# A gated linear recurrence on Trainium2: its in-block products as 32-column tiles of the TensorE array

## The chip, the cores and the metric

The kernel runs on one core of a Trainium2 chip. A core has a matrix engine (TensorE; PE in the profile, with its weight loads shown separately as PEld), a vector engine (VectorE, DVE), a scalar engine (ScalarE, ACT), a general engine (GpSimd, POOL) and a queue that issues DMAs (SyncE, SP). Each engine works through its own list of instructions in order and waits on semaphores for the others. The metric is the device time of one execution in microseconds (us), the median of the runs.

## The reference, cut to what matters

The kernel computes one layer of a diffusion backbone for 1024 latent and 128 context tokens of width 1024: a half-step SwiGLU network, a token mixer, a second half-step SwiGLU network and a final norm. The mixer adds attention and a bidirectional gated linear recurrence (HGRN2) with 8 heads of 64 x 64 state:

```
S_t = diag(f_t) S_{t-1} + k_t outer v_t        k_t = 1 - f_t
o_t = S_t^T q_t
```

It runs once forward and once backward over the latent tokens, each from a cached start state, and once over the context tokens from zero. The reference does it in chunks: inside a chunk the products are

```
A[t, s] = sum_k  decay(s -> t)[k] q[t, k] k[s, k]     (s <= t forward, s >= t backward)
o_intra[t] = sum_s A[t, s] v[s]
dS = sum_s (k[s] decayed to the chunk's end) outer v[s]
```

and between chunks the state goes on as `S <- diag(g) S + dS`, with `o_inter[t] = (q[t] decayed from the chunk's start) S`.

## The kernel before, in words

All matrix data stands feature-major: 128 features on the partitions, the 1152 tokens (1024 latent, 128 context) along the free axis, cut into three column groups of 384, taken in the order `ORDER = (2, 0, 1)`. The large dense products split every fp32 operand into a high and a low part and run three matmuls for it (`mm3`, lines 446 to 448; one record each). Small products stay in plain fp32; the profile shows each of these as two weight loads and two matmul records, except transposes, which are one of each.

The work goes: `start` and `ffn_fast` (first SwiGLU), `hgrn` (recurrence, with the dense projections that feed it and others woven in), `attn`, `merge`, and `ffn_fast` again. The change is in `hgrn` alone.

For each of the 8 heads the recurrence keeps forward data on partitions 0 to 63 (slice `A`) and backward data on 64 to 127 (slice `B`). One head has three units of 384 tokens, each of three blocks of 128 tokens. So there are 24 units. A unit is worked in two generators.

`scan_pre` makes keys and queries relative to blocks of 8 tokens (`Kb`, `Qb`), and `KE` and `QP`, their versions decayed to the ends of the 8-token blocks.

`scan_lev` then makes the 128 x 128 matrix of `A[s, t]` of each of the three blocks.

- First the 8-token blocks: line 858 multiplies `Kb` by `Qb` over the forward rows (a contraction of 64) into one PSUM tile of the tag `lv` and over the backward rows into another, three matmuls of 128 x 128 each. Line 859 copies what an 8-block mask lets through into `A1` and `A2` (VectorE, `copy_predicated`, 128 x 384).
- Then four levels m = 8, 16, 32, 64. `key_half` (lines 864 and 865, ScalarE) copies the left-half keys of each pair of m-blocks for forward and the right-half keys for backward into `kr`, whose other halves are zero. Line 873 multiplies `kr` by `QP` over all 128 rows, three matmuls of 128 x 128. Line 884 moves `KE` (two VectorE instructions) and `QP` (one GpSimd, one VectorE) on to blocks of 2m, and line 885 the factors `T`. For m < 64, line 888 copies what the mask of this level lets through from PSUM into `A1`; for m = 64, lines 890 and 891 copy the two off-diagonal quarters (ScalarE).
- Line 895 adds `A1` and `A2` to `Af` (VectorE, 128 x 384). Line 899 transposes `KE`, line 901 copies that out of PSUM, line 905 multiplies it by all 128 columns of `V` (two heads' values) and line 906 keeps the 64 of this head as `dS`.

After the three units of a head, `scan_out` runs the state through the blocks (line 916, 14 VectorE instructions) and then, for each unit, accumulates `V^T Af` (line 924) and `S^T QP` (line 928) into a PSUM tile `po`, on those 64 partitions that belong to the head, and copies them out (line 929).

Every generator yields between its steps. The loop in `hgrn` takes, at each yield of `scan_lev` or `scan_out`, one step of dense projection work (twelve matmuls of lines 446 to 448) and one step of `scan_pre` of the next unit. So TensorE's list reads: a small group of the recurrence, twelve dense matmuls, the next small group, and so on. A scheduler then settles the final order of each engine's list. PSUM tiles: the tag `lv` has three buffers, `sm` (transposes, `dS`, `po`) three and `mm` (dense) two.

Of the kernel before, what the change touches and what calls it, by code (L numbers as in the profile page):

```python
# [9 lines left out]
F32 = mybir.dt.float32  # L10
F32R = mybir.dt.float32r
BF16 = mybir.dt.bfloat16
U8 = mybir.dt.uint8
# [6 lines left out]
P = 128  # L20
# [6 lines left out]
CW = 384  # L27
# [3 lines left out]
ORDER = (2, 0, 1)  # L31
FINAL = (768, 1152), (0, 512), (512, 768)
H = 8
EPS = 1e-6
# [53 lines left out]
class Trunk:  # L88
# [515 lines left out]
    def mixer_consts(self, cp):  # L604
        nc, a = self.nc, self.a
        self.mask = cp.tile([P, 5, P], U8, name="mask")
        mf = self.tt(F32, "maskf")[:, : 5 * P]
        nc.scalar.dma_start(mf, a["mask"])
# [98 lines left out]
    def hgrn(self):  # L707
        nc = self.nc
# [3 lines left out]
        f32 = lambda n, sh: self.fp.tile(sh, F32, name=n)  # L712
        A, B = slice(0, 64), slice(64, P)
        self.kr = {m: [f32(f"kr{m}_{i}", [P, CW]) for i in range(1)] for m in (8, 16, 32, 64)}
# [3 lines left out]
        for m in self.kr:  # L718
            for t in self.kr[m]:
                nc.vector.memset(t, 0.0)  # L720
        for t in self.XY:
            nc.vector.memset(t[:, :, 3:4], 1.0)
        for t in self.A1 + self.A2:
# [37 lines left out]
        d = scan_of(0)  # L761
# [24 lines left out]
    def tmp(self, n, bufs=1, sh=(P, CW)):  # L786
        return self.fp.tile(list(sh), F32, tag=n, bufs=bufs, name=n)
# [48 lines left out]
    def scan_lev(self, d, b):  # L836
        nc = self.nc
# [9 lines left out]
        dS = d["dS"]  # L847
        A1, A2 = self.A1[self.cnt % 2], self.A2[0]
        self.cnt += 1
        Kb, Qb, KE, Tm = d["pre"]  # L850
        bc = lambda t, m: t.unsqueeze(2).to_broadcast([t.shape[0], t.shape[1], m])
        qp = QP[:, c0 : c0 + CW]
        lv = lambda: self.pp.tile([P, 3, P], F32, tag="lv", bufs=3, name="lv")
        mb = lambda i: self.mask[:, i].unsqueeze(1).to_broadcast([P, 3, P])
        for r, dst, mi in ((A, A1, 0), (B, A2, 1)):
            ps = lv()
            for j in range(3):
                nc.tensor.matmul(ps[:, j], Kb[r, ts(j, P)], Qb[r, ts(j, P)], start=True, stop=True)
            nc.vector.copy_predicated(dst, mb(mi), ps)
# [9 lines left out]
        for li, m in enumerate((8, 16, 32, 64)):  # L869
            kr = self.kr[m][0]  # L870
            ps = lv()
            for j in range(3):
                nc.tensor.matmul(ps[:, j], kr[:, ts(j, P)], qp[:, ts(j, P)], start=True, stop=True)
            tv = Tm.rearrange("p (n h) -> p n h", h=2)
# [11 lines left out]
            if m < 64:  # L886
                key_half(2 * m)
                nc.vector.copy_predicated(A1, mb(2 + li), ps)
            else:
                nc.scalar.copy(A1[A, :, B], ps[A, :, B])  # L890
                nc.scalar.copy(A1[B, :, A], ps[B, :, A])
            Tm = Tn
            yield
        Af = tmp("Af", 4, (P, 3, P))
        nc.vector.tensor_add(Af, A1, A2)
        d["As"][b] = Af
        pt = self.pp.tile([P, 3, P], F32, tag="sm", bufs=3, name="kt")
# [4 lines left out]
        yield  # L902
        pd = self.pp.tile([P, 3, P], F32, tag="sm", bufs=3, name="dS")
        for j in range(3):
            nc.tensor.matmul(pd[:, j], kT[:, j], V[:, ts(3 * b + j, P)], start=True, stop=True)
        nc.scalar.copy(dS[:, 3 * b : 3 * b + 3], pd[:, :, 64 * hh : 64 * hh + 64])
        yield

    def scan_out(self, d):
# [9 lines left out]
        r = slice(off, off + 64)  # L919
        for b in ORDER:  # L920
            po = self.pp.tile([P, 3, P], F32, tag="sm", bufs=3, name="po")
            for j in range(3):
                t = 3 * b + j
                nc.tensor.matmul(
                    po[r, j], V[:, t * P + off : t * P + off + 64], d["As"][b][:, j], start=True, stop=(t == 8)
                )
                if t < 8:
                    nc.tensor.matmul(po[r, j], S[:, t], QP[:, ts(t, P)], start=False, stop=True)
            nc.scalar.copy(d["o"][r, b * CW : (b + 1) * CW], po[r].rearrange("p a b -> p (a b)"))
            yield  # L930
# [836 lines left out]
def mask_table():  # L1767
    import numpy as np

    s, t = np.arange(P)[:, None], np.arange(P)[None, :]  # L1770
    same = lambda b: s // b == t // b
    m = [same(8) & (s <= t), same(8) & (s >= t)]
    m += [same(2 * b) & ~same(b) for b in (8, 16, 32)]
    return np.concatenate(m, 1).astype(np.float32)
# [35 lines left out]
```

## Time and profile before

| | |
|---|---|
| Runs | 2983.42, 2985.15, 2987.38 us; median 2985.15 |
| Profiled execution | 2987.2 us from its first to its last instruction; the page gives no other time for it |
| Mean granted TensorE clock | 0.987 |
| TensorE matmul busy | 2879.0 us (96%), 18498 records |
| TensorE weight loads busy | 2739.4 us (92%) |
| VectorE / ScalarE / GpSimd busy | 2026.6 / 1238.5 / 1029.7 us |
| The recurrence's stage | about 886 to 1508 us of the span |

Busy time of an engine is a union of its records, and matmul records overlap: a record of line 446 lasts about 0.34 us while the next starts 0.175 us after it. What a small group costs is therefore read from start to start in the timeline, not from the length of records.

### The profile page before, as it was taken

Reading aid. Unit: us, or ns where it says so; the run is one execution under the profiler, and the core shown is the slowest. Engines: PE = TensorE matmul, PEld = TensorE weight load, DVE = VectorE, ACT = ScalarE, POOL = GpSimd, SP = SyncE. Lnnn points to the kernel's source line nnn. Section 1 sums busy time; section 2 is a strip of 40 time slices with the busy share of each in tenths; the row PEclk is TensorE's granted clock in tenths of the full one; section 3 lists DMA queues with packets and bytes.
Section 4 is the critical chain, followed back from the end, with each engine's and each line's share of the span. In section 5 each row is a group of like instructions: output and inputs, shape, how many; then the busy total and the mean of one; then the engine's idle time right before and its main releaser. Section 6 shows DMA issues by size and latency. Waiting matters only on the chain. (4 is left out here: it accounts for less than half of the span.)

```text
span 2987.2 us, 49338 instructions
## 1 busy us (share of the span) xinstructions
PE 2879.0 (96%) x18498; PEld 2739.4 (92%) x18498; DVE 2026.6 (68%) x4238; ACT 1238.5 (41%) x2374; POOL 1029.7 (34%) x939
## 2 busy tenths in 40 slices
PE   6999999999989999999998999989999999999998
PEld 5999999999979989898997777779999999999997
DVE  7677777677677777878456677756674665546665
ACT  6432332321364555555244777731462233232112
POOL 0223223453243333323244445532342322226431
PEclk9999999999999999999998999999999999999999
DMA  6643433743121111111110000242352322235211
GB/s 242 205 142 120 133 121 118 265 138 116 63 64 56 38 44 38 54 38 51 60 48 12 16 15 25 62 161 82 123 176 94 106 88 75 74 110 210 91 45 64
DMA packets 151470, 282.37 MB, mean 95 GB/s; under 512 B 19200, under 2 KB 83648, under 8 KB 151232
## 3 DMA queue, kind: packets, MB, share of 16 engines
q1 hardware_dynamic: 151088, 278.90, 28.3%
q8 instruction: 146, 2.39, 0.3%
q14 instruction: 92, 0.75, 0.1%
q10 hardware_dynamic: 144, 0.33, 0.0%
HBM read 215.64 MB, written 63.52 MB: 93 GB/s over the span
## 5 line engine op out<-in xcount | busy, mean ns | idle before, releaser
L1560 PE MATMUL b<-xo,wo 128*128 128x288 f32 x3552 | 484.8, 296 | 0.0
L1560 PEld LDWEIGHTS b<-xo,wo 128*128 128x128 f32 x3552 | 476.6, 188 | 0.0
L475 DVE SCALAR_TENSOR_TENSOR x<-dn,modt,x 128x256 f32<-128x256 f32 (+4 forms) x728 | 353.4, 505 | 169.2 <-PE dn L448 168.1
L235 POOL TENSOR_TENSOR wl<-raw,wh 128x1024 fp32r<-128x1024 f32 (+1 forms) x106 | 235.4, 2222 | 418.7 <-ACT wh L234 353.0
L1560 PE MATMUL b<-bh,wo 128*128 128x288 f32 x1776 | 365.9, 295 | 0.8 <-ACT et L1570 0.8
L446 PE MATMUL mm<-xh,wh 128*128 128x384 f32 (+1 forms) x1008 | 360.5, 358 | 6.1 <-DVE q L665 4.1
L448 PE MATMUL mm<-xh,wl 128*128 128x384 f32 (+1 forms) x1008 | 342.2, 340 | 2.1 <-POOL wl L235 1.9
L447 PE MATMUL mm<-xl,wh 128*128 128x384 f32 (+1 forms) x1008 | 342.0, 339 | 0.0
L1560 PEld LDWEIGHTS b<-bh,wo 128*128 128x128 f32 x1776 | 289.1, 188 | 1.0 <-ACT et L1570 1.0
L1560 PE MATMUL b<-bl,wo 128*128 128x288 f32 x888 | 261.7, 295 | 0.0
L234 ACT CAST wh<-raw 128x1024 fp32r<-128x1024 f32 (+1 forms) x108 | 104.3, 968 | 257.2 <-PE dn L447 165.8
L1535 ACT CAST wo<-raw 128x512 fp32r<-128x512 f32 x185 | 114.7, 621 | 229.0 <-PE b L1560 116.9
L446 PEld LDWEIGHTS mm<-xh,wh 128*128 128x128 f32 (+1 forms) x1008 | 190.2, 189 | 16.0 <-DVE q L665 4.9
L446 PE MATMUL dn<-hh,wh 128*128 128x384 f32 (+2 forms) x576 | 196.3, 341 | 2.0 <-DVE x L475 1.1
L1536 DVE TENSOR_TENSOR wo<-raw,wo 128x512 fp32r<-128x512 f32 x185 | 127.1, 688 | 103.3 <-ACT wo L1535 100.3
L448 PE MATMUL dn<-hh,wl 128*128 128x384 f32 (+2 forms) x576 | 194.7, 338 | 1.0 <-POOL wl L235 1.0
L447 PE MATMUL dn<-hl,wh 128*128 128x384 f32 (+2 forms) x576 | 194.2, 337 | 0.0
L448 PEld LDWEIGHTS mm<-xh,wl 128*128 128x128 f32 (+1 forms) x1008 | 189.7, 188 | 3.6 <-POOL wl L235 2.2
L447 PEld LDWEIGHTS mm<-xl,wh 128*128 128x128 f32 (+1 forms) x1008 | 190.4, 189 | 1.7 <-issue 0.4
L1638 POOL TENSOR_TENSOR hl<-hr,hh 128x1152 fp32r<-128x1152 f32 x44 | 117.9, 2689 | 197.1 <-ACT hh L1637 105.8
L1292 POOL TENSOR_TENSOR ehl<-e,ehl 128x512 fp32r<-128x512 f32 x93 | 122.1, 1318 | 143.8 <-ACT ehl L1290 83.6
L306 DVE SCALAR_TENSOR_TENSOR junk<-wada,cb 128x512 bf16<-128x512 f32 x224 | 165.9, 741 | 5.3 <-DMA wada<-in_w_aT 4.5
(388 smaller groups left out, 7125.0 us busy)
## 6 DMA issues: line engine op xcount, KB each, us to landing
raw<-in_w SPq DMA_DIRECT2D x148, 256.0 KB, 2.9
raw<-in_w SPq DMA_DIRECT2D x58, 512.0 KB, 3.7
wada<-in_w_aT SPq DMA_DIRECT2D x112, 256.0 KB, 2.8
hr<-hs SPq DMA_DIRECT2D x44, 576.0 KB, 5.6
hs<-et SPq DMA_DIRECT2D x148, 144.0 KB, 1.8
raw<-in_w_in SPq DMA_DIRECT2D x41, 512.0 KB, 3.6
hb<-hd SPq DMA_DIRECT2D x44, 288.0 KB, 3.2
x<-in_xT SPq DMA_DIRECT2D x16, 576.0 KB, 6.2
```

The lines of the kernel that those rows point to most:

```text
L234: pin(self.nc.scalar.copy(wh, raw))
L235: pin((eng or self.nc.gpsimd).tensor_sub(wl, raw, wh))
L306: nc.vector.scalar_tensor_tensor(junk, ws[n % 2], 1.0, cs[s], ALU.mult, ALU.mult, accum_out=o)
L446: pin(nc.tensor.matmul(ps, wh, xh, start=start and i == 0, stop=False))
L447: pin(nc.tensor.matmul(ps, wh, xl, start=False, stop=False))
L448: pin(nc.tensor.matmul(ps, wl, xh, start=False, stop=stop and i == n - 1))
L475: nc.vector.scalar_tensor_tensor(self.x[m][:, a:b], ps[:, a - lo : b - lo], self.modt[:, gm, m, s : s + 1], self.x[m][:, a:b], ALU.mult, A ...
L1292: eng.tensor_sub(el, e, eh)
L1535: nc.scalar.copy(wh, src[i])
L1536: nc.vector.tensor_sub(wl, src[i], wh)
L1560: nc.tensor.matmul(ps, w[:, k], x[:, k, :QW], start=first, stop=last, skip_group_check=home != i)
L1638: nc.gpsimd.tensor_sub(hl, raw, hh)
```

## The change

- `mixer_consts`, `mask_table`: with the new constant `G = 32`, the masks are four of 128 x 32 in place of five of 128 x 128; column c of row s stands for token 32 * (s // 32) + c.
- `scan_lev`, products inside 32-token blocks (the 8-blocks and the levels 8 and 16): a new helper `products` issues, for each of the three blocks of 128, a 32 x 32 matmul for each of the four 32-token diagonal blocks, with the output on that block's own 32 partitions. For the 8-blocks it does so for the forward rows and the backward rows in turn, into two PSUM tiles.
- Levels 32 and 64: only the blocks that hold results are multiplied, forward over rows `A` into one `lv` tile and backward over rows `B` into another: at level 32 four matmuls of 32 x 32 per block of 128, at level 64 two of 64 x 64. The keys' zero halves are no longer needed there, so only `kr8` and `kr16` are cleared at the start.
- The masked copies and `A1`, `A2` shrink to 128 x 96, and the sum becomes `Ad` (128 x 96). `Af` is filled by ScalarE copies: four of 32 x 96 from `Ad` after level 16, four of 32 x 96 from PSUM at level 32, two of 64 x 192 at level 64.
- `dS`: two 64-column weight halves by the 64 columns of `V` of this head, into the two halves of one PSUM tile.
- `scan_out`: two PSUM tiles for nine blocks in place of three. In each, some blocks go to partitions 0 to 63 and others to 64 to 127, issued alternately; the order of blocks is 3, 4, 2, 5 and then 1, 6, 0, 7, 8. Four copies per head bring them out in place of three, and there is one yield less.

```diff
@@ mixer_consts
-        self.mask = cp.tile([P, 5, P], U8, name="mask")
+        self.mask = cp.tile([P, 4, G], U8, name="mask")
...
@@ hgrn
-        self.A1 = [f32(f"A1_{i}", [P, 3, P]) for i in range(2)]
-        self.A2 = [f32("A2", [P, 3, P])]
+        self.A1 = [f32(f"A1_{i}", [P, 3, G]) for i in range(2)]
+        self.A2 = f32("A2", [P, 3, G])
...
@@ scan_lev
+        Af = d["As"][b] = tmp("Af", 4, (P, 3, P))
...
-        lv = lambda: self.pp.tile([P, 3, P], F32, tag="lv", bufs=3, name="lv")
-        mb = lambda i: self.mask[:, i].unsqueeze(1).to_broadcast([P, 3, P])
-        for r, dst, mi in ((A, A1, 0), (B, A2, 1)):
-            ps = lv()
-            for j in range(3):
-                nc.tensor.matmul(ps[:, j], Kb[r, ts(j, P)], Qb[r, ts(j, P)], start=True, stop=True)
-            nc.vector.copy_predicated(dst, mb(mi), ps)
+        lv = lambda: self.pp.tile([P, 3, 64], F32, tag="lv", bufs=3, name="lv")
+        mb = lambda i: self.mask[:, i].unsqueeze(1).to_broadcast([P, 3, G])
+
+        def products(parts, k, q, blocks):
+            for j in range(3):
+                kj, qj = k[:, ts(j, P)], q[:, ts(j, P)]
+                for ki, qi in blocks:
+                    for r, ps in parts:
+                        ks, qs = (ki, qi) if r != B else (qi, ki)
+                        n = qs.stop - qs.start
+                        nc.tensor.matmul(ps[ks, j, :n], kj[r, ks], qj[r, qs], start=True, stop=True)
+
+        diag = [slice(u, u + G) for u in range(0, P, G)]
+        diag = list(zip(diag, diag))
+        pair = (A, lv()), (B, lv())
+        products(pair, Kb, Qb, diag)
+        for dst, mi, (_, ps) in zip((A1, A2), (0, 1), pair):
+            nc.vector.copy_predicated(dst, mb(mi), ps[:, :, :G])
...
         for li, m in enumerate((8, 16, 32, 64)):
-            kr = self.kr[m][0]
-            ps = lv()
-            for j in range(3):
-                nc.tensor.matmul(ps[:, j], kr[:, ts(j, P)], qp[:, ts(j, P)], start=True, stop=True)
+            kr = self.kr[m]
+            if m < G:
+                ps = lv()
+                products([(slice(0, P), ps)], kr, qp, diag)
+            else:
+                pair = (A, lv()), (B, lv())
+                blocks = [(slice(u, u + m), slice(u + m, u + 2 * m)) for u in range(0, P, 2 * m)]
+                products(pair, kr, qp, blocks)
...
             if m < 64:
                 key_half(2 * m)
-                nc.vector.copy_predicated(A1, mb(2 + li), ps)
+            if m < G:
+                nc.vector.copy_predicated(A1, mb(2 + li), ps[:, :, :G])
             else:
-                nc.scalar.copy(A1[A, :, B], ps[A, :, B])
-                nc.scalar.copy(A1[B, :, A], ps[B, :, A])
+                for u, v in blocks:
+                    nc.scalar.copy(Af[u, :, v], pair[0][1][u, :, :m])
+                    nc.scalar.copy(Af[v, :, u], pair[1][1][v, :, :m])
+            if m == 16:
+                Ad = tmp("Ad", 2, (P, 3, G))
+                nc.vector.tensor_add(Ad, A1, A2)
+                for u, _ in diag:
+                    nc.scalar.copy(Af[u, :, u], Ad[u])
             Tm = Tn
             yield
-        Af = tmp("Af", 4, (P, 3, P))
-        nc.vector.tensor_add(Af, A1, A2)
-        d["As"][b] = Af
...
-        pd = self.pp.tile([P, 3, P], F32, tag="sm", bufs=3, name="dS")
+        pd = self.pp.tile([P, 3, 64], F32, tag="sm", bufs=3, name="dS")
         for j in range(3):
-            nc.tensor.matmul(pd[:, j], kT[:, j], V[:, ts(3 * b + j, P)], start=True, stop=True)
-        nc.scalar.copy(dS[:, 3 * b : 3 * b + 3], pd[:, :, 64 * hh : 64 * hh + 64])
+            for r in (A, B):
+                v = V[:, (3 * b + j) * P + 64 * hh : (3 * b + j) * P + 64 * hh + 64]
+                nc.tensor.matmul(pd[r, j], kT[:, j, r], v, start=True, stop=True)
+        nc.scalar.copy(dS[:, 3 * b : 3 * b + 3], pd)
...
@@ scan_out
-        for b in ORDER:
+        for pairs, lows, highs in (((3, 4), (2, 5)), (2, 4), (4, 6)), (((1, 6), (0, 7), (8,)), (0, 2), (6, 9)):
             po = self.pp.tile([P, 3, P], F32, tag="sm", bufs=3, name="po")
-            for j in range(3):
-                t = 3 * b + j
-                nc.tensor.matmul(
-                    po[r, j], V[:, t * P + off : t * P + off + 64], d["As"][b][:, j], start=True, stop=(t == 8)
-                )
-                if t < 8:
-                    nc.tensor.matmul(po[r, j], S[:, t], QP[:, ts(t, P)], start=False, stop=True)
-            nc.scalar.copy(d["o"][r, b * CW : (b + 1) * CW], po[r].rearrange("p a b -> p (a b)"))
+            at = lambda t: po[A, t - lows[0]] if t < lows[1] else po[B, t - highs[0]]
+            for pair in pairs:
+                for t in pair:
+                    w = V[:, t * P + off : t * P + off + 64]
+                    nc.tensor.matmul(at(t), w, d["As"][t // 3][:, t % 3], start=True, stop=(t == 8))
+                for t in pair:
+                    if t < 8:
+                        nc.tensor.matmul(at(t), S[:, t], QP[:, ts(t, P)], start=False, stop=True)
+            for half, (t0, t1) in ((A, lows), (B, highs)):
+                pv = po[half, : t1 - t0].rearrange("p a b -> p (a b)")
+                nc.scalar.copy(d["o"][r, t0 * P : t1 * P], pv)
             yield
```

In the built program a unit's five product groups hold 24, 12, 12, 12 and 6 matmuls in place of 6, 3, 3, 3 and 3, `dS` has 6 in place of 3, and a head's outputs keep 17. ScalarE's list has ten `Af` copies per unit in place of the two of lines 890 and 891. The dense matmuls, the loads and the stores are the same in number.

More of the change, by code (lines that the diff above doesn't have):

```diff
@@ L32 @@
 FINAL = (768, 1152), (0, 512), (512, 768)
+G = 32
 H = 8
@@ L605, in mixer_consts @@
         nc, a = self.nc, self.a
[L606 to L607 removed]
+        self.mask = cp.tile([P, 4, G], U8, name="mask")
+        mf = self.tt(F32, "maskf")[:, : 4 * G]
         nc.scalar.dma_start(mf, a["mask"])
@@ L713, in hgrn @@
         A, B = slice(0, 64), slice(64, P)
-        self.kr = {m: [f32(f"kr{m}_{i}", [P, CW]) for i in range(1)] for m in (8, 16, 32, 64)}
+        self.kr = {m: f32(f"kr{m}", [P, CW]) for m in (8, 16, 32, 64)}
         self.XY = [f32(n, [P, 48, 8]) for n in "XY"]
-        self.A1 = [f32(f"A1_{i}", [P, 3, P]) for i in range(2)]
-        self.A2 = [f32("A2", [P, 3, P])]
-        for m in self.kr:
-            for t in self.kr[m]:
-                nc.vector.memset(t, 0.0)
+        self.A1 = [f32(f"A1_{i}", [P, 3, G]) for i in range(2)]
+        self.A2 = f32("A2", [P, 3, G])
         for t in self.XY:
             nc.vector.memset(t[:, :, 3:4], 1.0)
-        for t in self.A1 + self.A2:
+        for t in self.A1 + [self.A2, self.kr[8], self.kr[16]]:
             nc.vector.memset(t, 0.0)
@@ L1768, in mask_table @@
     import numpy as np
-    s, t = np.arange(P)[:, None], np.arange(P)[None, :]
+    s = np.arange(P)[:, None]
+    t = s // G * G + np.arange(G)[None, :]
     same = lambda b: s // b == t // b
     m = [same(8) & (s <= t), same(8) & (s >= t)]
-    m += [same(2 * b) & ~same(b) for b in (8, 16, 32)]
+    m += [same(2 * b) & ~same(b) for b in (8, 16)]
     return np.concatenate(m, 1).astype(np.float32)
```

4 lines of the change are left out of this document (2 added, 2 removed).

## The prediction

> **What bounds the kernel now.** I read the page's totals, then the busy times of the recurrence's stage, its TensorE groups and waits, then timelines. First the page's totals; then stage rows (start:end, length, busy time of PE, PEld, DVE, ACT, POOL, granted clock): the stage and two heads of it.
>
> ```profile
> span 2987.2 us, 49338 instructions
> PE 2879.0 (96%) x18498; PEld 2739.4 (92%) x18498; DVE 2026.6 (68%) x4238; ACT 1238.5 (41%) x2374; POOL 1029.7 (34%) x939
> ```
>
> ```profile
> 1197.00:1275.00 78.00, 72.99 (x446) 67.87 (x445) 62.02 (x135) 43.76 (x90) 25.06 (x31) 0.98 0.15 50
> 1275.00:1352.00 77.00, 75.49 (x487) 71.48 (x486) 58.39 (x130) 40.39 (x86) 24.02 (x29) 1.00 0.13 40
> 886.00:1508.00 622.00, 593.42 (x3742) 558.37 (x3742) 456.60 (x1003) 319.55 (x668) 194.13 (x228) 0.99 0.15 49
> ```
>
> TensorE is busy for 593 of the stage's 622 us, VectorE for 457, ScalarE for 320. So TensorE's list sets the end, and a microsecond taken from it counts while the others keep up. The stage's waits of TensorE, by total and times:
>
> ```profile
> PE lv L873 <- DVE QP L884: 17.3, 15, 2.3
> PE lv L873 <- POOL QP L884: 4.9, 6, 1.2
> PE vt L678 <- ACT t L675: 4.3, 4, 2.0
> ```
>
> Some 22 of the 29 idle microseconds are the level products waiting for `QP`.
>
> **The prices of small groups.** A group's price is the distance from the dense matmul before it to the second after it, less two dense matmuls (0.175 us apart, as the first three rows show). Timeline rows, start and length:
>
> ```profile
> 1041.44 0.33 PE L446 MATMUL mm<-xh,wh 128*128 128x384 f32 x1
> 1041.61 0.34 PE L447 MATMUL mm<-xl,wh 128*128 128x384 f32 x1
> 1041.79 0.34 PE L448 MATMUL mm<-xh,wl 128*128 128x384 f32 x1
> 1041.97 0.83 PE L873 MATMUL lv<-QP,kr 128*128 128x128 f32 x6
> 1042.55 0.42 PE L446 MATMUL mm<-xh,wh 128*128 128x384 f32 x1
> 1042.82 0.34 PE L447 MATMUL mm<-xl,wh 128*128 128x384 f32 x1
> ...
> 1083.34 0.34 PE L448 MATMUL mm<-xh,wl 128*128 128x384 f32 x1
> 1083.61 1.26 PE L858 MATMUL lv<-Qb,Kb 64*128 64x128 f32 x12
> 1084.80 0.44 PE L446 MATMUL mm<-xh,wh 128*128 128x384 f32 x1
> 1085.08 0.34 PE L447 MATMUL mm<-xl,wh 128*128 128x384 f32 x1
> ```
>
> ```profile
> 1029.55 0.34 PE L448 MATMUL mm<-xh,wl 128*128 128x384 f32 x1
> 1029.82 0.43 PE L924 MATMUL po<-Af,V 128*64 128x128 f32 x2
> ...
> 1030.52 0.38 PE L928 MATMUL po<-QP,S 128*64 128x128 f32 x2
> 1030.74 0.38 PE L924 MATMUL po<-Af,V 128*64 128x128 f32 x2
> 1031.05 0.44 PE L446 MATMUL mm<-xh,wh 128*128 128x384 f32 x1
> 1031.33 0.34 PE L447 MATMUL mm<-xl,wh 128*128 128x384 f32 x1
> ```
>
> - A level group (L873): 1042.82 - 1041.79 - 0.35 = 0.68 us for 6 records, 0.113 each. `dS` (L905) has the same form, so the same price.
> - The 8-block group (L858): 1.74 - 0.35 = 1.39 us.
> - An output group: 1.78 - 0.35 = 1.43 us for ten records. They start 0.22 us apart by twos, 0.11 each, 1.10 in all. The other 0.33 us is the change of tile shape, there and back: the level group, whose shape is that of the dense matmuls, has none of it.
>
> So the change adds a shape change to the levels 8 to 64 and to `dS`, 0.33 us each, five times in a unit.
>
> **Do column tiles overlap?** The one place with 32-column tiles is line 251, four matmuls of 256 columns on four tiles; beside it a row with whole-array records of 384:
>
> ```profile
> 23.82 2.37 PE L251 MATMUL adap<-wada,sc 128*32 128x256 f32 x40
> 1044.73 2.10 PE L936 MATMUL ops<-osq,onesb 128*128 128x384 f32 x6
> ```
>
> L936 takes about 0.32 us a record ((2.10 - 0.49) / 5), so 0.215 per 256 columns. Forty in a row would take 8.6 us; they took 2.37, ten rounds of 0.215 and a tail. Four tiles cost what one costs, so I let tiles overlap.
>
> **Can the instructions come fast enough?** A 32 x 32 record should hold its tile for a quarter of 0.11, 0.028 us (estimate), so the number of instructions matters: each record comes with a weight load, and a unit's six groups go from 42 records to 144. Two semaphore waits in TensorE's sequencer bound its pace (events of line 928 in the window 1109.5 to 1112, first and last start; then weight loads of the timeline):
>
> ```profile
> L928 PEldq EVENT_SEMAPHORE  x2: 51/51/51, 1110.8 to 1111.5; - x2
> ```
>
> ```profile
> 1111.40 0.19 PEld L928 LDWEIGHTS po<-QP,S 128*64 128x64 f32 x2 [0.22 <-DVE S L916]
> 1111.57 0.25 PEld L924 LDWEIGHTS po<-Af,V 128*64 128x64 f32 x2
> ...
> 1114.29 0.19 PEld L924 LDWEIGHTS po<-Af,V 128*64 128x64 f32 x2 [0.25 <-issue]
> 1114.45 0.25 PEld L928 LDWEIGHTS po<-QP,S 128*64 128x64 f32 x2
> ```
>
> Between the two events stand 36 instructions (three small matmuls of four, twelve dense of two), passed in 0.7 us: at most 0.0194 us each. The second event belongs to the L928 load of 1114.45, so the sequencer ran 2.9 us, some 32 instructions, ahead and stood there. I take 32 as waiting when a group starts and 0.015 us for each further one, nearer the bound than to nothing, since this row is the only one that times the sequencer.
>
> [...]
>
> **The sum, per unit.**
> - 8-blocks: 24 matmuls, 96 instructions. 0.33 + 64 x 0.015 = 1.29 for 1.39: -0.10.
> - Levels 8 and 32: 12 matmuls, 48 instructions. 0.33 + 16 x 0.015 = 0.57 for 0.68: -0.11 each.
> - Level 16 still waits for two engines at once, and one of these waits stands in the sequencer. 21 of the 72 groups of levels 16 to 64 had such idle time (15 and 6 above). In 3 of 10 I let nothing be queued, 0.33 + 48 x 0.015 = 1.05; on average 0.71: +0.03.
> - Level 64 and `dS`: 12 records on two tiles of 64, six times 0.055 on each, 0.66 with the shape change: -0.02 each.
>
> That is -0.33 us, over 24 units -8 us. Bounds: nothing queued and 0.0194 each gives 2.19, three times 1.26 and twice 0.80, +2.78 a unit, +67 us; tiles alone setting the pace gives 0.50 (six records of 0.028 on each) for the four groups with 32-column tiles, -1.47 a unit, -35 us.
>
> **Outputs, per head.** Now 34 records of 0.11 and three shape changes, 4.73 us. The third group runs straight into the 8-blocks:
>
> ```profile
> 1036.84 0.34 PE L448 MATMUL mm<-xh,wl 128*128 128x384 f32 x1
> ...
> 1038.56 1.26 PE L858 MATMUL lv<-Qb,Kb 64*128 64x128 f32 x12
> ...
> 1040.04 0.34 PE L447 MATMUL mm<-xl,wh 128*128 128x384 f32 x1
> ```
>
> 3.20 - 0.35 = 2.85 for 1.65 + 1.39 = 3.04, so 0.19 is saved there, and 4.54 stand. After: 16 records in two halves, 8 x 0.11, then 18 with ten on one half, 10 x 0.11, and two shape changes: 2.64. That is -1.9, over 8 heads -15 us; without overlap -1 us.
>
> **The other engines.** Prices (count, busy, mean ns):
>
> ```profile
> L859 DVE COPY_PREDICATED A<-mask,lv 128x384 f32<-128x384 uint8 x48 | 25.5, 577 | 68.7 <-PE lv L858 68.3
> L888 DVE COPY_PREDICATED A<-mask,lv 128x384 f32<-128x384 uint8 x72 | 42.6, 592 | 2.1
> L895 DVE TENSOR_TENSOR Af<-A,A 128x384 f32<-128x384 f32 x24 | 15.1, 628 | 1.7 <-ACT A L891 1.5
> L890 ACT COPY A<-lv 64x192 f32<-64x192 f32 x24 | 7.5, 311 | 11.7 <-PE lv L873 11.4
> L901 ACT COPY kT<-kt 128x384 f32<-128x384 f32 x24 | 11.5, 478 | 9.8 <-PE kt L899 9.7
> L643 ACT ACT_TABLE_LOAD x9 | 11.5, 1283 | 0.1
> ```
>
> VectorE: six instructions, 2 x 0.577 + 3 x 0.592 + 0.628 = 3.56 us, become five of a quarter the width, about 0.25 each by my estimate (a quarter would be 0.15, the rest is for what does not shrink): some 55 us less over the stage. It lies beside TensorE, but shortens the 17.3 us that the products wait for `QP`: 0 to -17, taken as -3. ScalarE: eight more copies; a line through 311 ns (192 wide) and 478 (384) gives 0.23 us at 96, so +1.9 us a unit, +45 us on 320. Hidden by TensorE except in one place: three `lv` buffers now serve eight tiles a unit instead of six, so level 64's second tile waits for three copies of level 32, 0.7 us. Twelve dense matmuls, 2.1 us, cover that unless ScalarE is 1.4 us late, as behind a table load of 1.28. Queued behind that wait stand the dense matmuls. 0 to +24 (1 us a unit), taken as +3. Smaller masks, clearings, DMAs: nothing on this path.
>
> Sum: -8 - 15 - 3 + 3 = -23 on 2987.2, 2964 for the profiled execution. That one stands 2.0 us above the median 2985.15, so 2962 for the median. Its own range is 2950 to 2976.
>
> **Rivals.**
> - *More*: the queue always suffices and the tiles set the pace. For it the 32 instructions ahead, against it groups of 96. 2985 - 35 - 15 = 2935.
> - *Slower*: groups find an empty queue, since so many semaphore waits stand in the sequencer. At 0.015 with nothing queued: 8-blocks 1.77, three levels 1.05, two groups 0.69, +1.5 a unit, +36 us, less 15: 3006, and 3037 at 0.0194. It decides once about half of the groups start unfed (+15 us). For it the 21 waits; against it the long run ahead at L928.
> - *No change*: ScalarE's copies come late at level 64 in every unit, +24: 2986. For it is the fixed price of small copies, against it 300 idle microseconds of ScalarE. [...]
> - *Tiles do not overlap* in these shapes: 48 x 0.028 for the 8-blocks, 24 x 0.028 for a level, 12 x 0.055 for the others, +1.9 a unit; with the outputs' -1, 3029. Against it L251.
>
> **Chances.** Forecast 0.53, more 0.18, slower 0.15, no change 0.11, no overlap 0.03. The range 2932 to 3006 leaves out the last case, over half of "slower", whose times run from 3006 to 3037, and a quarter of "more": some 0.17. The likeliest case's own range is given above. Beyond 0.2% (6 us, about what runs of this kernel can tell): faster 0.71 (the first two), same 0.11, slower 0.18.
>
> **What would show it.** In the profile after: the first matmuls of an 8-block group nanoseconds apart and the rest paced by the sequencer; a group of level 8 at 0.57 and the 8-blocks at 1.29 by the measure above; output groups at 1.21 and 1.43; `copy_predicated` near 0.25 us; the stage some 23 us shorter than 622. Wrong if a level group costs over 0.9 us, or if a wait for ScalarE at level 64 adds up to over 15 us.

## The result

| | median, us | profiled execution, span |
|---|---|---|
| before | 2986.27 (2983.42 to 2990.96) | 2987.2 |
| after | 2958.61 (2957.45 to 2961.18) | 2959.4 |

The ratio is 0.9907, with a 95% interval of 0.9893 to 0.9921. The kernel is 27.7 us faster, beside 23 predicted.

Below, the stage runs from the first to the last matmul of the recurrence. Its row is start:end, length, busy time of PE, PEld, DVE, ACT, POOL, clock. First the kernel before, then the changed one:

```profile
885.71:1500.50 614.79, 586.21 (x3706) 551.96 (x3705) 456.31 (x1003) 312.57 (x660) 192.17 (x228) 0.99 0.15 47
```

```profile
888.66:1474.52 585.86, 548.22 (x6142) 487.73 (x6141) 421.22 (x968) 355.16 (x852) 190.97 (x223) 0.98 0.15 52
```

The stage is 28.9 us shorter, so all of the gain lies in it. TensorE is busy 38.0 us less, but idle 37.6 us instead of 28.6: of the 38, 9 were lost to waiting. The waits of the changed kernel's TensorE in the stage (total, times, longest):

```profile
PE lv L862 <- ACT Af L906: 14.4, 9, 3.0
PE lv L862 <- POOL QP L898: 10.3, 8, 1.3
PE lv L862 <- DVE QP L898: 3.5, 7, 0.6
```

Where `QP` from VectorE was 17.3 us before, it is 3.5 now, and a wait for ScalarE's copies of level 32 (`Af`, line 906) has come in.

A second loss goes with the waits. The granted clock in the stage row is 0.98, where it was 0.99, and it is not spread evenly. It stands at 0.50 for 3.4 or 6.8 us at a time, twice in the stage before (6.8 us in all) and five times in the changed one (23.9 us, from 891.6, 1048.6, 1198.8, 1349.0 and 1393.4). The second of these, a row of the same kind, and dense matmuls from it:

```profile
1048.63:1055.45 6.82, 5.61 (x22) 5.40 (x23) 5.04 (x10) 5.42 (x15) 1.90 (x3) 0.50 0.08 30
```

```profile
1053.71 0.52 PE L449 MATMUL mm<-xh,wl 128*128 128x384 f32 x1
1054.03 0.52 PE L447 MATMUL mm<-xh,wh 128*128 128x384 f32 x1
```

Dense matmuls start 0.32 us apart there, elsewhere 0.175. In each of the five cases TensorE had stood idle for 1.5 to 3.0 of the 3.4 us before. Not every such wait has this effect: one of 2.3 us at 1089.9 in the kernel before had none. By the two distances, 0.45 of TensorE's busy time in these stretches is lost, some 10 us in the changed kernel and 3 in the one before (estimates from one execution each).

The prices of the groups, by the prediction's measure (from the dense matmul before a group to the second one after it, less 0.35). From the changed kernel's timeline, an output group, an 8-block group, a level group, then (earlier and later) `dS` and level 64:

```profile
1020.22 0.34 PE L449 MATMUL mm<-xh,wl 128*128 128x384 f32 x1
1020.48 0.57 PE L925 MATMUL dS<-V,kT 128*64 128x64 f32 x12
1020.98 0.45 PE L447 MATMUL mm<-xh,wh 128*128 128x384 f32 x1
1021.27 0.34 PE L448 MATMUL mm<-xl,wh 128*128 128x384 f32 x1
...
1028.43 0.34 PE L449 MATMUL mm<-xh,wl 128*128 128x384 f32 x1
1028.71 0.44 PE L946 MATMUL po<-Af,V 128*64 128x128 f32 x4
...
1029.95 0.45 PE L447 MATMUL mm<-xh,wh 128*128 128x384 f32 x1
1030.23 0.34 PE L448 MATMUL mm<-xl,wh 128*128 128x384 f32 x1
...
1031.98 0.34 PE L449 MATMUL mm<-xh,wl 128*128 128x384 f32 x1
1032.25 0.62 PE L862 MATMUL lv<-Qb,Kb 64*32 64x32 f32 x48
1032.80 0.44 PE L447 MATMUL mm<-xh,wh 128*128 128x384 f32 x1
1033.09 0.34 PE L448 MATMUL mm<-xl,wh 128*128 128x384 f32 x1
...
1034.84 0.34 PE L449 MATMUL mm<-xh,wl 128*128 128x384 f32 x1
1035.11 0.40 PE L862 MATMUL lv<-QP,kr 128*32 128x32 f32 x24
1035.43 0.44 PE L447 MATMUL mm<-xh,wh 128*128 128x384 f32 x1
1035.71 0.34 PE L448 MATMUL mm<-xl,wh 128*128 128x384 f32 x1
...
1044.65 0.34 PE L449 MATMUL mm<-xh,wl 128*128 128x384 f32 x1
1044.92 0.56 PE L862 MATMUL lv<-QP,kr 64*64 64x64 f32 x6
1045.41 0.44 PE L447 MATMUL mm<-xh,wh 128*128 128x384 f32 x1
1045.68 0.34 PE L448 MATMUL mm<-xl,wh 128*128 128x384 f32 x1
```

| group | before | predicted | measured (undisturbed groups) |
|---|---|---|---|
| 8-blocks | 1.39 | 1.29 | 0.75 |
| levels 8, 16 and 32 | 0.68 | 0.57, 0.71, 0.57 | 0.53 |
| level 64 | 0.68 | 0.66 | 0.69 |
| `dS` | 0.68 | 0.66 | 0.70 |
| outputs, 16 and 18 records | 4.54 a head | 1.21 and 1.43 | 1.22 and 1.44 |

In these prices a unit's products save 1.39 + 5 x 0.68 - (0.75 + 3 x 0.53 + 0.69 + 0.70) = 1.06 us, 25 us in 24 units, and the outputs 1.88 us a head, 15 us. Of these 40 us the lower clock takes back some 7, and TensorE's busy time in the stage fell by 38; the difference of 5 us, of which some 2 are a dozen other records fewer in that window, is otherwise not accounted for.

### The profile page after: what moved, and what is told of

Read it like the earlier page. It is cut to its first block, busy times and chain, and to the rows that moved or that the text cites. A ratio compares the mean times of both kernels' runs of the same rounds, so it can differ in the third digit from the quotient of the medians.

```text
span 2959.4 us, 54352 instructions
## 1 busy us (share of the span) xinstructions
PE 2839.9 (96%) x20946; PEld 2674.2 (90%) x20946; DVE 1993.1 (67%) x4212; ACT 1285.5 (43%) x2574; POOL 1035.0 (35%) x939
## 5 line engine op out<-in xcount | busy, mean ns | idle before, releaser
L235 ACT CAST wh<-raw 128x1024 fp32r<-128x1024 f32 (+1 forms) x108 | 104.3, 968 | 244.0 <-PE dn L448 168.2
L1554 POOL TENSOR_TENSOR ws<-raw 128x256 f32<-128x256 f32 x74 | 70.1, 966 | 292.8 <-DMA raw<-in_w 263.2
```

Of the source, the lines that this page charges most:

```text
L235: pin(self.nc.scalar.copy(wh, raw))
L1554: nc.gpsimd.tensor_tensor(o[:, c], x[:, c], y[:, c], op)
```

## The experiments

Each ratio is to the kernel before, run beside it on the same chip; the medians of before differ by up to 3 us from one set of runs to another, so small differences between two kernels are read from the ratios. "Idle" is the stage's length less TensorE's busy time in it, from one row of that kind for each kernel; "half clock" is the time in the stage at a granted clock of 0.50, in the same execution. The kernel before has 28.6 and 6.8.

| kernel | median, us | ratio to before, 95% interval | stage, us | idle, us | half clock, us |
|---|---|---|---|---|---|
| after | 2958.61 | 0.9907 (0.9893 to 0.9921) | 585.9 | 37.6 | 23.9 |
| outputs only | 2976.73 | 0.9972 (0.9963 to 0.9981) | 602.4 | 31.7 | 13.7 |
| products only | 2965.30 | 0.9931 (0.9918 to 0.9943) | 595.0 | 30.5 | 17.1 |
| levels 32 and 64 whole | 2958.32 | 0.9911 (0.9896 to 0.9926) | 583.1 | 40.2 | 6.8 |
| level 32's copies on VectorE | 2974.00 | 0.9958 (0.9946 to 0.9971) | 600.1 | 48.2 | 30.7 |
| masked copies three times | 2973.62 | 0.9956 (0.9943 to 0.9968) | 600.3 | 48.4 | 27.3 |
| 8-blocks twice | 2960.20 | 0.9914 (0.9900 to 0.9927) | 587.0 | 33.4 | 13.7 |
| level 64 whole | 2956.57 | 0.9901 (0.9887 to 0.9914) | 582.7 | 40.6 | 17.1 |
| the same, sum on GpSimd | 2957.90 | 0.9903 (0.9888 to 0.9918) | 582.9 | 40.5 | 17.1 |
| outputs, narrow copies, old products | 2981.32 | 0.9979 (0.9970 to 0.9988) | 607.7 | 33.0 | 23.9 |
| products twice | 2993.96 | 1.0020 (1.0011 to 1.0029) | 614.9 | 29.4 | 23.9 |
| after, weights' low parts in pieces | 2950.99 | 0.9874 (0.9859 to 0.9889) | 575.4 | 31.8 | 10.2 |
| before, weights' low parts in pieces | 2984.97 | 0.9996 (0.9987 to 1.0005) | 613.6 | 26.1 | 10.2 |

### Each half of the change alone

The new `scan_out` in the kernel before; and the changed kernel with the old `scan_out`.

```diff
-        for b in ORDER:
+        for pairs, lows, highs in (((3, 4), (2, 5)), (2, 4), (4, 6)), (((1, 6), (0, 7), (8,)), (0, 2), (6, 9)):
...
```

> The kernel before with the change of the outputs alone. Theory (a group's price is a gain of the path): the output groups fall from 4.54 us to 2.64 us a head as they did in the changed kernel (1.22 and 1.44 there), 8 x 1.9 = 15 us, so 2986 - 15 = 2971. Rival (the state's VectorE chain or the copies of po set the pace of this place, so that faster matmuls only wait): 2983 or more.

> The changed kernel with the outputs of before. Theory (the parts add up): changed kernel 2959 + 15 = 2974, that is -12 on before; TensorE's idle time at level 64 behind ScalarE's copies of level 32 stays (14 us in the changed kernel). Rival (the two parts share a gain, since both relieve the same engine): 2963 or less.

The outputs alone gave 9.7 us, the products alone 21.1, 30.8 together beside the 27.7 of both. In the kernel with the outputs alone the two output groups cost 1.22 and 1.44 us in all 16 places, and TensorE is busy 15.5 us less, as the theory had it. But its waits for `QP`:

```profile
PE lv L873 <- DVE QP L884: 19.5, 15, 2.5
PE lv L873 <- POOL QP L884: 6.0, 7, 1.2
```

were 17.3 and 4.9 before. Idle time rose by 3.1 us though nothing of the products had been touched, and the time at half clock by 6.9, which is some 3 us more. So the two theories each missed by a part: neither is the sum exact, nor do the parts share a large gain. Each part gives less than its price. That a shorter list of TensorE reaches the waits for the other engines sooner fits these rows; it is argued from them, not tried by itself.

### Is it ScalarE that level 64 waits for?

Levels 32 and 64 as whole products into one `lv` tile (six tiles a unit); then level 64 alone (seven).

```diff
-                pair = (A, lv()), (B, lv())
...
-                products(pair, kr, qp, blocks)
+                ps = self.pp.tile([P, 3, P], F32, tag="lv", bufs=3, name="lv")
...
+                products([(slice(0, P), ps)], kr, qp, [(slice(0, P), slice(0, P))])
```

> The changed kernel with the levels 32 and 64 multiplied as before, three whole 128 x 128 products of kr and QP into one lv tile; the ten ScalarE copies of a unit stay. A unit then takes six lv tiles, so level 64 no longer waits for the copies of level 32. Theory (the wait comes from lv tiles that stand behind ScalarE's list, 14.4 us): -14, and +0.15 us for level 32 in 24 units, +3.6; 2959 - 11 = 2948. Rival (ScalarE is late for everything at that place, so TensorE waits for the next thing, the keys kr or the transposes' copy kT): 2959 + 3 = 2962.

```diff
-            if m < G:
-                ps = lv()
-                products([(slice(0, P), ps)], kr, qp, diag)
+            if m < G or m == 64:
+                ps = self.pp.tile([P, 3, P], F32, tag="lv", bufs=3, name="lv")
+                products([(slice(0, P), ps)], kr, qp, diag if m < G else [(slice(0, P),) * 2])
```

> The changed kernel with level 64 alone multiplied as before (three whole products into one lv tile, 0.68 us where the two halves take 0.69), level 32 left on column tiles. A unit takes seven lv tiles, and level 64 no longer needs a tile that level 32's copies hold. If those copies are what it waits for (14.4 us in the changed kernel): 2945. If they only hide that QP comes late from VectorE (with levels 32 and 64 whole, 17 us more of waits for QP took the place of the 14.4): 2955 to 2959, the lower end by the 3.6 us that whole products of level 32 cost there.

The wait for `Af` was gone in both, and the time stayed (2958.3 and 2956.6; the intervals of both ratios hold the changed kernel's 0.9907), as the second theory for level 64 alone had it. The wait for VectorE's `QP` with levels 32 and 64 whole:

```profile
PE lv L862 <- DVE QP L898: 20.8, 16, 2.8
```

`QP` from VectorE has come back to 20.8 us, where the changed kernel shows 3.5. So the row "`lv` <- ACT `Af` 14.4" names the last of two late things. The longest of these waits in the changed kernel's timeline shows both:

```profile
1048.83 0.60 DVE L898 TENSOR_TENSOR QP<-QP,T 64x192 f32<-64x192 f32 x1
...
1049.55 0.23 ACT L906 COPY Af<-lv 32x96 f32<-32x96 f32 x1
...
1049.84 0.90 PE L862 MATMUL lv<-QP,kr 64*64 64x64 f32 x6 [2.95 <-ACT Af L906]
```

VectorE's part of `QP` ended at 1049.43, and the copy that let the tile go at 1049.78. Of the 2.95 us only 0.35 are ScalarE's. The theory of the 14.4 us fell; the rival that I had given, a wait that moves to another ScalarE instruction, fell too: it is VectorE's.

### Does VectorE's load matter?

Two ways to give VectorE work back in the changed kernel: level 32's four copies on VectorE; and each masked copy three times.

```diff
-                for u, v in blocks:
-                    nc.scalar.copy(Af[u, :, v], pair[0][1][u, :, :m])
-                    nc.scalar.copy(Af[v, :, u], pair[1][1][v, :, :m])
+                for (u, v), cp in zip(blocks, [nc.vector.tensor_copy if m == G else nc.scalar.copy] * 2):
+                    cp(Af[u, :, v], pair[0][1][u, :, :m])
+                    cp(Af[v, :, u], pair[1][1][v, :, :m])
```

> The changed kernel with the four copies of level 32 out of PSUM on VectorE instead of ScalarE. Theory (ScalarE's list is what level 64's second tile waits for): the 14.4 us go, VectorE gets 96 x 0.25 = 24 us of work back, of which up to 6 us return as waits for QP: 2945 to 2951. Rival (the wait only moves to the next ScalarE instruction): 2957 to 2961.

```diff
-            nc.vector.copy_predicated(dst, mb(mi), ps[:, :, :G])
+            [nc.vector.copy_predicated(dst, mb(mi), ps[:, :, :G]) for _ in range(3)]
...
-                nc.vector.copy_predicated(A1, mb(2 + li), ps[:, :, :G])
+                [nc.vector.copy_predicated(A1, mb(2 + li), ps[:, :, :G]) for _ in range(3)]
```

> The changed kernel with each of its four predicated copies of a unit made three times over (the same values again). VectorE gets 24 x 8 x 0.26 = 50 us of work back, TensorE's list is not changed. Prediction's theory (VectorE's relief was worth 3 us, 17 at most): 2959 + 3 = 2962, to 2975. New theory (VectorE's chain sets TensorE's idle time: with level 32's copies on it 27 us more work cost 15): 2959 + 28 = 2987, so the whole gain would be gone. Rival to both (those 15 us were lv tiles held behind VectorE, which here wait as well): between 2965 and 2975.

Both came out 15 us slower than the changed kernel, where I had expected a gain of 8 to 14 from the first. For the second, the theory that VectorE's chain would take back the whole gain (2987) fell; 2973.6 lies in the rival's range (`lv` tiles held longer behind VectorE), and just under the prediction's upper bound. Their stage rows, the first kernel's and the second's:

```profile
889.59:1489.68 600.09, 551.84 (x6142) 491.05 (x6141) 447.99 (x1064) 332.36 (x756) 190.91 (x223) 0.97 0.15 51
```

```profile
891.53:1491.83 600.30, 551.85 (x6142) 490.31 (x6141) 444.84 (x1160) 355.53 (x852) 191.23 (x223) 0.98 0.16 51
```

TensorE's busy time is the changed kernel's to within 4 us, and for these 4 it has more time at half clock (30.7 and 27.3 us for 23.9). VectorE's is 448 and 445 instead of 421, and TensorE's idle time 48 instead of 38. The second kernel had 50 us of copies added and only 24 more of busy time: records that overlap count once, and other instructions became shorter by 13 us together. Rows of its waits and, first, one of the kernel with the copies on VectorE:

```profile
PE lv L862 <- DVE Af L906: 11.2, 13, 1.6
```

```profile
PE lv L862 <- ACT Af L906: 20.7, 14, 3.2
PE lv L862 <- DVE QP L898: 12.2, 12, 1.6
```

In the first, 11.2 us are waits for an `lv` tile that VectorE's own copies hold; in the second, both the wait for a tile and the wait for `QP` have grown (14.4 and 3.5 before). So behind the faster products some 25 us more of VectorE's work cost 15 us of the kernel; how much of that is late `QP` and how much held tiles was not separated. The prediction's 3, with 17 as its bound, was the low end.

The counterpart: the narrow copies without the faster products.

```diff
-            nc.vector.copy_predicated(dst, mb(mi), ps)
+            nc.vector.copy_predicated(dst[:, :, :32], mb(mi)[:, :, :32], ps[:, :, :32])
...
-                nc.vector.copy_predicated(A1, mb(2 + li), ps)
+                nc.vector.copy_predicated(A1[:, :, :32], mb(2 + li)[:, :, :32], ps[:, :, :32])
```

> The kernel before with the outputs in two halves and with its five predicated copies of a unit cut to the first 32 of the 128 columns, so that the other three quarters of those copies are left out; every product is made as before. VectorE is relieved of 120 x 0.32 = 39 us, TensorE has no faster products. If VectorE's work sets TensorE's idle time by itself, at the price of the changed kernel (50 us for 15): 2977 - 12 = 2965; at the dearer price of level 32's copies (27 us for 15): 2955. If relief counts only behind faster products, or is worth what the prediction took for it (3): 2973 to 2977.

This kernel leaves out what the other three quarters of the copies bring, and serves for its time alone. It gained nothing: 2981.3, beside 2976.7 for the same kernel with wide copies, and the intervals of the two overlap. VectorE was busy 37 us less (426.5 for 463.7) and TensorE's idle time did not fall (33.0 for 31.7), while the time at half clock rose from 13.7 to 23.9. Why is seen where the longest waits lie. VectorE's timeline at one of them, wide copies first and narrow ones behind:

```profile
1044.42 0.59 DVE L888 COPY_PREDICATED A<-mask,lv 128x384 f32<-128x384 uint8 x1
1046.91 1.02 DVE L355 SCALAR_TENSOR_TENSOR rt<-ops,osq 128x384 f32<-128x384 f32 x2 [1.89 <-ACT osq L354]
...
1051.88 0.36 DVE L884 TENSOR_TENSOR QP<-QP,T 64x192 f32<-64x192 f32 x1
```

```profile
1046.33 0.27 DVE L888 COPY_PREDICATED A<-mask,lv 128x96 f32<-128x96 uint8 x1
1048.91 1.02 DVE L355 SCALAR_TENSOR_TENSOR rt<-ops,osq 128x384 f32<-128x384 f32 x2 [2.31 <-ACT osq L354]
...
1053.88 0.35 DVE L884 TENSOR_TENSOR QP<-QP,T 64x192 f32<-64x192 f32 x1
```

The part of `QP` that the next product needs stands in VectorE's list behind the norm of the outputs (`rec_norm`, lines 355 to 357), which waits for ScalarE. The narrow copy is 0.32 us shorter, and VectorE waits 0.42 us longer for ScalarE. Here the time taken from VectorE ahead of a wait of its own was lost. For the other places this is not shown.

### Does TensorE's list still set the end?

```diff
-        products(pair, Kb, Qb, diag)
+        [products(pair, Kb, Qb, diag) for _ in range(2)]
```

> The changed kernel with the 24 matmuls of the 8-blocks issued twice over in each unit, 48 records and 96 instructions more on TensorE in 24 units, each into the same place. If the tiles set the pace (six records of 0.028 us on each, 0.17 a unit): +4 us, 2963. If the sequencer sets it once its queue is empty, at the pace of the last 16 records of an 8-block group in the changed kernel (0.27 us for 16 records, 0.0167 each): 48 x 0.0167 = 0.80 a unit, +19 us, 2978. With the prediction's 0.015 us per instruction: 1.44 a unit, +35 us, 2994. The gain of fewer idle microseconds, if the group covers waits: up to -5 on each.

```diff
-                        nc.tensor.matmul(ps[ks, j, :n], kj[r, ks], qj[r, qs], start=True, stop=True)
+                        [nc.tensor.matmul(ps[ks, j, :n], kj[r, ks], qj[r, qs], start=True, stop=True) for _ in range(1 + (n < 64))]
```

> The changed kernel with every product on 32-column tiles (8-blocks, levels 8, 16 and 32) issued twice, which gives TensorE back about what the change saved it: 0.40 + 3 x 0.20 = 1.0 us a unit, 24 us, while VectorE's copies stay narrow. If TensorE's list sets the end, as the prediction took it: 2959 + 24 = 2983. If VectorE's chain sets the stage's pace, so that the added time only fills idle time (8-blocks twice: 9.6 us added, 1.6 seen): 2962 to 2966. Taken with the copies three times over (2974) and the kernel with old products and new outputs (2977), the second would say that the faster products alone were worth some 3 to 8 us, and the narrow copies the rest.

An 8-block group of the first kernel:

```profile
1034.12 0.34 PE L449 MATMUL mm<-xh,wl 128*128 128x384 f32 x1
1034.39 1.02 PE L862 MATMUL lv<-Qb,Kb 64*32 64x32 f32 x96
1035.34 0.44 PE L447 MATMUL mm<-xh,wh 128*128 128x384 f32 x1
1035.62 0.34 PE L448 MATMUL mm<-xl,wh 128*128 128x384 f32 x1
```

It costs 1.15 us, 0.40 more for 48 records and their loads: 8.3 ns a record, 4.2 ns an instruction. That is half of what I had expected from the queue's empty end and a fourth of the prediction's 0.015 an instruction. Only 1.6 of these 9.6 us reached the time, and the intervals can't tell that from nothing. But with all four groups doubled the time rose by 35 us. There each matmul stands twice in a row on its own tile, and that is dearer: an 8-block group of 96 records costs 1.29 and not 1.15, and a level group of 48 records costs 0.85, where 48 on eight tiles cost 0.75. The prices are 24 x (0.54 + 3 x 0.32) = 36 us, not the 24 expected, and the stage row says:

```profile
890.24:1505.09 614.85, 585.44 (x9022) 525.55 (x9021) 410.22 (x968) 358.22 (x852) 188.87 (x223) 0.98 0.16 50
```

TensorE is busy 37.2 us more and idle 8.2 less, and the stage is 29.0 us longer (the profiled execution, 2989.3, was the fastest of its eleven). So TensorE's list does set the end, and my theory of a VectorE chain that swallows TensorE's time fell. That the 8-blocks twice cost so little is seen in the table: against the 9.6 us stand 4.2 us less of idle time and 10.2 us less at half clock, worth some 4 to 5 us, and the stage is 1.2 us longer. VectorE's busy time is the same (420 us for 421). Line 817's product of `qx` and `Y` (next part) took 585 ns instead of 1287, but line 816's of `kk` and `X`, just ahead of it, 1147 instead of 634. Why the waits became shorter was not tried.

### Who holds VectorE?

Groups of VectorE in the changed kernel's stage (count, busy, mean ns), the first of them in the kernel before (line 819 there), and a piece of the changed kernel's timeline with GpSimd:

```profile
L817 DVE TENSOR_TENSOR Qb<-qx,Y 64x384 f32<-64x384 f32 x22 | 28.3, 1287 | 0.3
...
L817 DVE TENSOR_TENSOR Qb<-qx,X 64x384 f32<-64x384 f32 x22 | 12.2, 553 | 0.1
```

```profile
L819 DVE TENSOR_TENSOR Qb<-qx,Y 64x384 f32<-64x384 f32 x22 | 12.0, 544 | 0.1
```

```profile
998.20 2.52 POOL L236 TENSOR_TENSOR wl<-raw,wh 128x1024 fp32r<-128x1024 f32 x1 [2.71 <-ACT wh L235]
998.51 2.27 DVE L825 TENSOR_TENSOR T<-TK,TQ 128x48 f32<-128x48 f32 x1
```

Two products of one form take 1287 and 553 ns on average, and one of 48 columns took 2.27 us. It ended at 1000.78, just behind the GpSimd subtraction of line 236, which ended at 1000.72. The average of 1287 comes from seven of the 22 products: each began 0.40 us after such a subtraction, took 2.74 us and ended 0.41 us behind it. As I read these rows, the subtraction holds VectorE's instruction up until it ends; by what means, they do not show. So the subtraction was cut into four, in the recurrence alone, in the changed kernel and in the one before:

```diff
-        pin((eng or self.nc.gpsimd).tensor_sub(wl, raw, wh))
+        [pin((eng or self.nc.gpsimd).tensor_sub(wl[:, i], raw[:, i], wh[:, i])) for i in getattr(self, 'pieces', [slice(None)])]
...
-        self.cnt = 0
+        self.cnt, self.pieces = 0, [slice(i, i + 2) for i in range(0, 8, 2)]
...
-            oT, d = d["o"], nd
+            oT, d, self.pieces = d["o"], nd, [slice(None)] if h == H - 1 else self.pieces
```

> The changed kernel with GpSimd's subtraction of a weight's high part (128 x 1024, 2.3 us each) made in four pieces of 256 columns inside the recurrence. In the changed kernel a VectorE product of 48 columns took 2.27 us and ended with such a subtraction. If VectorE is held for as long as one GpSimd instruction lasts and gets in between two of them: VectorE's busy time in the stage falls by 15 us or more and the time by 5 to 10, 2949 to 2954. If it is held for the whole stretch in any case: 2957 to 2962, with the pieces' fixed cost on GpSimd.

> The kernel before with GpSimd's subtraction of a weight's high part in four pieces inside the recurrence, nothing else. In the changed kernel the same edit took 8 us. If single VectorE instructions that GpSimd holds up are what the products' waits for QP come from in this kernel too (17.3 us of waits for VectorE's part, 4.9 for GpSimd's): 2986 - 8 = 2978 or less. If the edit, like the narrow copies, is worth something only behind faster products: 2983 to 2988.

GpSimd's groups, of the changed kernel and of the one with the pieces:

```profile
L236 POOL TENSOR_TENSOR wl<-raw,wh 128x1024 fp32r<-128x1024 f32 x33 | 81.7, 2475 | 138.7 <-ACT wh L235 138.6
```

```profile
L236 POOL TENSOR_TENSOR wl<-raw,wh 128x256 fp32r<-128x256 f32 (+1 forms) x125 | 104.3, 864 | 131.8 <-ACT wh L235 131.7
```

The second row has some whole subtractions among the pieces, 864 ns on average over both. GpSimd works 23 us longer, and the kernel is 7.6 us faster, 2951.0; its interval (0.9859 to 0.9889) lies below the changed kernel's. VectorE's busy time fell by 8.5 us (412.7 for 421.2), not by 15: line 817's product of `qx` and `Y` takes 770 ns on average where it took 1287, but its product of `qx` and `X` 750 where it took 553. The waits for `Af` fell from 14.4 us to 12.4, the longest of them from 2.95 to 2.3; TensorE is idle 5.8 us less in all, and the time at half clock fell from 23.9 to 10.2 us, worth some 6 us more. GpSimd's own work does not come in earlier between the pieces, since the four stand together in its list. That the shorter instructions on VectorE are what shortened TensorE's waits is likely, but shown only by the edit as a whole.

In the kernel before, the same edit gave nothing, 0.9996, as the second theory had it. There line 819's product was never held, as its 544 ns show, and VectorE's busy time stayed at 456.3; other VectorE instructions do meet the subtraction there (line 827's product of `TK` and `TQ` takes 209 ns by its median and up to 2.76 us). So whether the edit needs faster products or only such a meeting is not shown.

Last, the sum `Ad` on GpSimd instead of VectorE, on top of level 64 whole:

```diff
-                nc.vector.tensor_add(Ad, A1, A2)
+                nc.gpsimd.tensor_add(Ad, A1, A2)
```

> The same with the sum Ad of A1 and A2 on GpSimd instead of VectorE, 24 x 0.26 = 6 us less of VectorE's work. If VectorE's chain costs half a microsecond for each of its own: 3 us less than the kernel with level 64 whole. If GpSimd, which makes a part of QP in each level (10.3 us of TensorE's waits are for it), is the later one: 2 to 5 us more.

2957.9 beside 2956.6 with overlapping intervals: neither theory's size is seen.

## Why the prediction held, point by point

The forecast (2962, range of the likeliest 2950 to 2976) holds the 2958.6, but its terms were not those of the run.

- **What bounds the kernel.** TensorE's list, as said: products twice put back 37 us and the stage grew by 29. What the sum has no term for is that the shorter list waited more (9 us) and that the granted clock fell behind long waits (some 7 us).
- **Outputs, -15.** The prices were right to 0.01 us. Taken alone they moved the time by 9.7 us. The term was mis-sized by what it leaves out: in that kernel TensorE waits 3.1 us more and has 6.9 us more at half clock.
- **Products, -8.** This is the step that failed. The prices give -25, and the kernel with the products alone, VectorE's and ScalarE's part included, gained 21. What was wrong is the sequencer's pace: 0.015 us for each instruction beyond 32 queued, read from two semaphore events. In the changed kernel's windows of line 862 alone, over the first 8-block group (start:end, length, PE and PEld busy with counts):

```profile
888.66:888.84 0.18, 0.18 (x32) 0.18 (x33) 1.00 0.91 296
888.84:888.89 0.05, 0.05 (x32) 0.05 (x16) 1.00 0.20 82
```

  Thirty-two records have started within 0.18 us, none starts in the next 0.05, and the rest follow. So the form was right, first from the queue and then at the sequencer's pace. But 32 records with their loads are 64 instructions, not 32, and the pace after them is 4.2 ns an instruction (8-blocks twice). By the first of these two rows a level group's 48 instructions would all fit, and its records start by fours, from the second on 0.032 us from one four to the next; 0.028 was the estimate for a tile's hold, so there the tiles may set the pace, as "more" had it. The bound had been an upper one: 36 instructions passed in at most 0.7 us, and I took a value near it without a row that said so.
- **The change of tile shape, 0.33.** It held: 0.53 for a level of 24 records, 0.75 for 48 and 1.15 for 96 lie on one line of 8.5 ns a record and 0.33 us beside them. The groups of products twice lie above that line (0.85 for 48, 1.29 for 96), so the 8.5 ns were measured only where neighbours go to different tiles.
- **Level 64 and `dS`, 0.66.** 0.69 and 0.70: no gain, as level 64 whole shows (2956.6).
- **VectorE's relief, -3.** Wrong as a term by itself: the narrow copies alone gave nothing, and with VectorE loaded again the faster products gave 3 us beyond the outputs (2973.6 for 2976.7), which the intervals can't tell from nothing. Both together gave 18 (2958.6). The kernel with the copies three times stands in here for one with wide copies, which was not run. So products and copies are one term, some -18 to -21, and the sum of the parts had no place for that.
- **ScalarE, +3.** The profile shows 14.4 us of waits for it, just under the 15 that I had named as fatal, and no time that the intervals can tell from nothing hangs on them (2956.6 with level 64 whole).
- **The rivals.** "More" was nearer on the products, though not on the time: the levels come close to the tiles' pace (0.53, where the tiles alone would give 0.50 by the prediction's estimate), the 8-blocks do not (0.75), and its 50 us of TensorE were 38, of which 9 were lost again. "No change" was right on the place of a new wait and wrong on its cause. "Slower" and "no overlap" did not happen.

So the time came out near by luck, because errors of opposite sign met: the products won 17 us more on TensorE than said, and against it stand 9 us of new idle time and some 7 us of lower clock, where the sum had -3 and +3.

## What to carry to other kernels

Cost a group's gain on the bounding engine, and then ask what the other engines' chains do when it reaches them sooner: here a quarter of TensorE's gain (9 of 38 us) came back as waiting, with more lost to the clock, which stood at 0.50 for 23.9 us behind long waits. Cheaper VectorE steps were worth nothing before TensorE was faster (2981.3 us beside 2976.7), and giving their work back afterwards cost 15 us. A wait row can name the last of several late things (ScalarE's part was 0.35 us of a wait of 2.95), so test it by removing that one thing before building on it. Where one engine's instruction takes several times its twin's duration (here 2.74 us beside 0.55), look for a long GpSimd instruction that ends at the same moment or just before, and try it in pieces: here that was worth 7.6 us in one kernel and nothing in the other.

## What was not expected of the hardware

- Forty-eight records of 32 x 32 on eight tiles took 0.42 us beside the change of shape, 8.5 ns each, and 24 on four tiles gave the same 8.5 ns a record. So more than four tiles at a time brought nothing here; why the two agree is not shown.
- TensorE took 64 instructions, 32 loads and 32 matmuls, at 0.18 us in all before its sequencer's pace showed.
- A VectorE instruction of 48 columns took 2.27 us while GpSimd's ran. GpSimd's subtraction in pieces of a quarter the width, some whole ones among them, took 864 ns an instruction instead of 2475, 104.3 us for 81.7 in all, and still the changed kernel gained 7.6 us.
- The granted clock was 0.97 to 0.99 in the stage in all of these kernels, but in the changed kernel it is 1.00 with five stretches of 0.50 that last 3.4 or 6.8 us, each behind 1.5 to 3.0 us of idle time of TensorE: 23.9 us of them in all, where the kernel before has 6.8 and the fastest one 10.2.
